# Summing four modulation rows over the partitions: matrix products with ones, or GpSimd additions with layout changes through DRAM

## The chip, the cores and the metric

The program runs on one core of one Trainium2 chip. The metric is the device time of one execution in microseconds (us), as the median of several. Before the change it is 1385.47 us, the median of 3 runs (1384.9 to 1385.56).

## What is computed

One layer of a diffusion backbone over 1024 latent tokens of width 1024, with 256 context tokens. A conditioning vector c gives six modulation rows of 1024 numbers each; two token mixers (retention and differential attention) share one input projection and one output projection; a gated MLP follows.

```python
sc = jax.nn.silu(c)
m_lat = sc @ w_mod + b_mod
sh1, sc1, g1, sh2, sc2, g2 = split(m_lat, 6)
h = rms_norm(x, norm1_g) * (1 + sc1) + sh1
y = token_mixers(h, h_ctx, w_in, ...) @ w_out
x = x + g1 * y
h2 = rms_norm(x, norm2_g) * (1 + sc2) + sh2
x = x + g2 * conv_ffn(h2, w_up, conv_w, conv_b, w_down)
return rms_norm(x, final_g)
```

The first two rows (sh1, sc1) are needed at once. This text is about the other four, the late ones: g1, sh2, sc2 and g2, numbered i = 0 to 3. Each is a product of a vector of 1024 with a matrix of 1024 x 1024.

## The kernel before

All matrix products in fp32 precision are made as three products of split operands (high x high, high x low, low x high; lines L131 to L133). A weight slice `raw` is loaded by SP's queue, ScalarE casts it to `whi` (L187), VectorE subtracts to get `wlo` (L188), and TensorE uses both.

**The stages near the change.** The input projection has seven column blocks of 512. They run in the order 6, 5, 2, 1, 3, 0, 4. Each block has four weight slices. Block 5 gives the keys of the attention (`transposed`, L450: tiles `pl`), block 2 the values of the retention (`natural`, L392: tiles `pn`, with a mean subtracted by three VectorE operations, L406 to L408), block 1 the retention keys, first for the two context tiles (`natural`, the last call before the change's new place) and then for the latents (`transposed`). `natural` leaves each tile in PSUM until ScalarE has copied it out (L403).

**The late modulation rows** are made beside blocks 5, 2 and 1 by the generator `modulations2` (L464), which is advanced from inside the matrix loops (`tick`). For each row i it loads eight tiles of weights `wm2` (128 partitions x 1024 columns) over SP's queue, with four buffers, and accumulates on VectorE: `macc = wm2 * silu(c) + macc` (L481). `macc` starts as zeros from a GpSimd memset (L478), with the bias row loaded by SP into its first partition (L479). There are two `macc` buffers. At the end `macc` holds 128 partial sums for each of 1024 columns, one for each partition.

**The sum over partitions** is `turned_sums` (L489). For i = 0 and 3 two products of a matrix of ones with `macc` (L494, `pg`, 128x512) give the summed row in all 128 partitions; ScalarE copies it out (L496) and SP stores it to DRAM as 128 equal rows (`g1_d`, `g2_d`, L497). For i = 1 and 2 eight products of `macc` with two columns of ones (L501, `pg`, 128x2) give the row as a column layout, one number for each partition and block of 128, which VectorE writes to the small tile `m2` (L503, L505, L506). Row i is summed when row i + 1 has had its fourth step; row 3 is summed at the end.

**Where the sums are used.** `g1` is loaded by GpSimd's queue during the attention (L1025) and used in the output projection; `m2` is used when the MLP's input is turned (`turned`, L1098); `g2bc` is loaded by SP's queue (L1429) and used at the end.

**What sets the order.** In these stages a scheduler lays out each engine's queue from a model of its own; each engine then runs its queue in that order and waits where an operand is late. In the attention, the order of all engines but GpSimd is written out by hand (a table of times for one unit of 128 queries and one head, 32 units), and `order_only` pins an instruction behind another. GpSimd's queue holds, besides the memsets above, nothing from the context tiles to the outputs of the retention (`score`, L246, whose first GpSimd operation is `qq`, L251), which run beside block 0.

Of the kernel before, what the change touches and what calls it, by code (L numbers as in the profile page):

```python
# [8 lines left out]
F32 = mybir.dt.float32  # L9
# [3 lines left out]
ALU = mybir.AluOpType  # L13
# [4 lines left out]
P = 128  # L18
D = 1024
KD = D // P  # L20
# [18 lines left out]
COL_N2 = 72  # L39
# [33 lines left out]
def kernel(  # L73
# [16 lines left out]
    nc = tc.nc  # L90
    mm = nc.tensor.matmul
# [17 lines left out]
    ones = kp.tile([P, P], F32, name="ones")  # L109
# [6 lines left out]
    def order_only(ins, before):  # L116
        tc.add_manual_dep(ins, before.name, mybir.DependencyInfo(mybir.DependencyClass.NoSync, mybir.DependencyReason.DATA), reason="order")
# [19 lines left out]
    g1_d = dr.tile([P, D], F32, name="g1d")  # L137
    g2_d = dr.tile([P, D], F32, name="g2d")
# [9 lines left out]
    m2 = kp.tile([P, 2, KD], F32, name="m2")  # L148
# [5 lines left out]
    with ExitStack() as p1:  # L154
# [5 lines left out]
        pst = psx.enter_context(tc.tile_pool(name="pst1", bufs=3, space=PSUM, side="right"))  # L160
# [11 lines left out]
        ev = p1.enter_context(tc.tile_pool(name="ev", bufs=2))  # L172
# [291 lines left out]
        def modulations2():  # L464

            def load(n):
                wt = m2p.tile([P, D], F32, name="wm2", bufs=4)
                tc.keep_in_program_order(nc.sync.dma_start(out=wt, in_=w_mod2[n // KD, n % KD]))
                return wt

            wts, acc, done = [], None, None
            for n in range(4 * KD + 3):
                if n < 4 * KD:
                    wts.append(load(n))
                i, k = divmod(n - 3, KD)
                if k == 0 and n >= 3:
                    done, acc = acc, m2p.tile([P, D], F32, name="macc", bufs=2)
                    nc.gpsimd.memset(acc, 0.0)  # L478
                    tc.keep_in_program_order(nc.sync.dma_start(out=acc[0:1, :], in_=rows[:, R_BMOD + (2 + i) * D : R_BMOD + (3 + i) * D]))  # L479
                if n >= 3:  # L480
                    nc.vector.scalar_tensor_tensor(out=acc, in0=wts.pop(0), scalar=csil[:, k, 0:1], in1=acc, op0=ALU.mult, op1=ALU.add)  # L481
                if k == 3 and i > 0:
                    turned_sums(i - 1, done)
                yield
            yield
            yield
            turned_sums(3, acc)

        def turned_sums(i, acc):  # L489
            if i in (0, 3):  # L490
                dst = g1_d if i == 0 else g2_d
                for n in range(2):
                    pg = pst.tile([P, 512], F32, name="pg", tag="tr")
                    mm(pg, ones, acc[:, n * 512 : (n + 1) * 512], start=True, stop=True)  # L494
                    st = ev.tile([P, 512], F32, name="st")
                    nc.scalar.copy(st, pg)  # L496
                    nc.sync.dma_start(out=dst[:, n * 512 : (n + 1) * 512], in_=st)  # L497
            else:
                pg = pst.tile([P, KD, 2], F32, name="pg2", tag="tr")
                for d in range(KD):  # L500
                    mm(pg[:, d, :], acc[:, d * P : (d + 1) * P], ones[:, 0:2], start=True, stop=True)  # L501
                if i == 1:
                    nc.vector.tensor_copy(m2[:, 0, :], pg[:, :, 0])  # L503
                else:
                    nc.vector.tensor_scalar(out=m2[:, 1, :], in0=pg[:, :, 0], scalar1=1.0, scalar2=None, op0=ALU.add)  # L505
                    nc.vector.tensor_tensor(out=m2[:, 1, :], in0=m2[:, 1, :], in1=cl[:, COL_N2 : COL_N2 + KD], op=ALU.mult)  # L506

        by_head = [(h, hf) for h in range(H) for hf in range(2)]
        m2c = p1.enter_context(ExitStack())
# [1 line left out]
        with ExitStack() as p0:  # L511
# [52 lines left out]
            part = [mm_tile("pn") for _ in range(4)]  # L564
# [95 lines left out]
            for k in range(KD):  # L660
# [28 lines left out]
                n = k + 4  # L689
# [87 lines left out]
        with tc.tile_pool(name="rc0", bufs=1) as r0:  # L777
# [20 lines left out]
            acc = r0.tile([P, 8], F32, name="acc")  # L798
# [30 lines left out]
        beside(iter(()), 0.0)  # L829
        pctx.close()  # L830
        m2c.close()
        rtab = load_rope(0)
        rtx = p1.enter_context(ExitStack())
        rt = rtx.enter_context(tc.tile_pool(name="rt", bufs=2, side="right"))
# [177 lines left out]
    with ExitStack() as p2:  # L1012
        at = p2.enter_context(tc.tile_pool(name="at", bufs=2))
        psa = p2.enter_context(tc.tile_pool(name="psa", bufs=1, space=PSUM))

        turns = {}
        start = len(nc.cur_bb.bb.instructions)
        order = sorted(TAU.items(), key=lambda it: it[1] % 1.0)
        for n in range(n_units + 8):
            if 1 < n < n_units:  # L1020
                units[n] = Unit(n)
                vars(units[n]).update(fore[n])
            if n == 9:
# [356 lines left out]
    with ExitStack() as p5:  # L1380
# [292 lines left out]
```

## Time and profile before

| | |
|---|---|
| median of 3 runs | 1385.47 us |
| the profiled execution | 1386.43 us |
| its span, first to last instruction | 1384.6 us |
| TensorE busy | 1366.8 us, 99% of the span |
| TensorE's clock in the profile | full in all 40 slices |
| VectorE, ScalarE, GpSimd busy | 998.1, 733.9, 302.0 us |
| HBM traffic | 154 GB/s over the span |

The profiled execution took 1386.43 us, 0.96 us more than the median; 1.8 us of it lie outside the span. Lines of the timeline read: start in us, duration in us, engine, line, operation, output <- inputs, shape, and in brackets how long the engine had been idle and who released it. A busy TensorE is modelled: matrix products overlap, so the distance between two starts is the cost of one and not its duration.

### The profile page before, as it was taken

To read this page: it belongs to the slowest core of one execution; us is meant where nothing else is said; L and a number is where in the kernel's file an instruction comes from. 1 tells how busy PE (TensorE), PEld (TensorE's weight loads), DVE (VectorE), ACT (ScalarE), POOL (GpSimd) and SP (SyncE) were. 2 spreads that over 40 slices of the span, in tenths; PEclk is the share of its full clock that TensorE was granted. 3 is DMA by queue.
4 is the path that set the end of the run, shared out by engine and by line. 5 is a ranking of instruction groups with operands and counts; after the bars stand their busy time and mean duration, and the time that the engine had idled before them with its cause. 6 is when DMAs were issued, how large, how long until landed. Compare 5 with 4: busy or idle time off the path is not lost.

```text
span 1384.6 us, 19518 instructions
## 1 busy us (share of the span) xinstructions
PE 1366.8 (99%) x7066; PEld 1149.8 (83%) x7066; DVE 998.1 (72%) x1474; ACT 733.9 (53%) x1400; POOL 302.0 (22%) x323
## 2 busy tenths in 40 slices
PE   9999999999999999999999999999999999999997
PEld 6788888888988799998888788888888888888886
DVE  4655874424776898896458998887778777799857
ACT  4652322434665789987136644555545555454534
POOL 1310000002666423411200643222332220000001
PEclk9999999999999999999999999999999999999999
DMA  9546885464564778622510232332323325963523
GB/s 361 215 163 209 299 269 178 144 177 147 153 190 140 217 176 184 143 52 78 190 67 24 98 109 106 114 114 92 114 99 114 107 69 178 378 226 111 179 91 122
DMA packets 95624, 214.63 MB, mean 155 GB/s; under 512 B 9316, under 2 KB 29796, under 8 KB 95016
## 3 DMA queue, kind: packets, MB, share of 16 engines
q1 hardware_dynamic: 86792, 187.03, 39.6%
q0 software_dynamic: 8160, 24.91, 7.9%
q10 hardware_dynamic: 576, 1.44, 0.3%
q8 instruction: 56, 0.92, 0.3%
q14 instruction: 40, 0.33, 0.1%
HBM read 158.03 MB, written 55.31 MB: 154 GB/s over the span
## 4 chain that ended last, share of the span: by engine, by line
PE 90%; DVE 3%; POOL 2%; ACT 2%; DMA 2%; issue 1%; POOLq 0%; SPq 0%; DVEq 0%; ACTq 0%
PE chain L131 6%; PE chain L132 6%; PE chain L133 6%; PE pv L906 5%; PE pA L874 5%; PE c L133 5%; PE c L131 5%; PE c L132 5%; PE pn L131 3%; PE pn L133 3%; PE pn L132 3%; PE pl L133 3%; PE pl L131 3%; PE pl L132 3%; PE third L131 3%; PE third L133 3%
## 5 line engine op out<-in xcount | busy, mean ns | idle before, releaser
L131 PE MATMUL pl<-hT,whi 128*128 128x512 f32 x256 | 105.7, 413 | 0.0
L131 PE MATMUL chain<-T,whi 128*128 128x512 f32 x264 | 103.0, 391 | 1.1 <-ACT ua L1306 1.1
L132 PE MATMUL chain<-T,whi 128*128 128x512 f32 x264 | 102.8, 389 | 0.0
L133 PE MATMUL chain<-T,wlo 128*128 128x512 f32 x264 | 102.4, 389 | 0.0
L133 PE MATMUL pl<-hT,wlo 128*128 128x512 f32 x256 | 100.3, 392 | 0.0
L132 PE MATMUL pl<-hT,whi 128*128 128x512 f32 x256 | 100.0, 391 | 0.0
L877 DVE TENSOR_REDUCE mt<-pA 128x1 f32<-128x1280 f32 x64 | 95.1, 1489 | 3.6 <-PE pA L874 3.2
L874 PE MATMUL pA<-ks,qhl 128*128 128x512 f32 (+1 forms) x384 | 89.7, 369 | 0.8 <-DMA ks<-dk 0.6
L131 PE MATMUL c<-whi,ghl 128*128 128x512 f32 x232 | 90.2, 389 | 0.0
L132 PE MATMUL c<-wlo,ghl 128*128 128x512 f32 x232 | 90.2, 389 | 0.0
L133 PE MATMUL c<-whi,ghl 128*128 128x512 f32 x232 | 90.2, 389 | 0.0
L881 ACT ACTIVATE p<-pA,mt 128x1280 f32<-128x1280 f32 x64 | 85.4, 1335 | 5.3 <-DVE mt L877 4.4
L1054 ACT CAST whi<-cmb 128x512 fp32r<-128x512 f32 x62 | 38.4, 622 | 81.8 <-PE chain L132 69.3
L874 PEld LDWEIGHTS pA<-ks,qhl 128*128 128x128 f32 x384 | 67.8, 189 | 13.3 <-issue 1.3
L906 PE MATMUL pv<-va,aT 128*128 128x128 f32 x640 | 77.0, 275 | 0.1
L1218 POOL TENSOR_TENSOR cmb<-wrb 128x512 f32<-128x512 f32 x19 | 27.9, 1468 | 221.9 <-DMA wrb<-w_up 168.9
L1057 DVE TENSOR_TENSOR wlo<-cmb,whi 128x512 fp32r<-128x512 f32 x62 | 60.1, 973 | 20.3 <-ACT whi L1054 20.3
L906 PEld LDWEIGHTS pv<-va,aT 128*128 128x128 f32 x640 | 74.0, 192 | 0.7 <-DVE yT L935 0.3
L1054 ACT CAST whi<-wra 128x512 fp32r<-128x512 f32 x54 | 33.2, 622 | 73.3 <-PE third L132 42.3
L131 PE MATMUL third<-yT,whi 128*128 128x512 f32 x168 | 65.4, 389 | 0.0
L132 PE MATMUL third<-yT,whi 128*128 128x512 f32 x168 | 65.4, 389 | 0.0
L133 PE MATMUL third<-yT,wlo 128*128 128x512 f32 x168 | 65.4, 389 | 0.0
(328 smaller groups left out, 3853.7 us busy)
## 6 DMA issues: line engine op xcount, KB each, us to landing
wm<-w_mod SPq DMA_DIRECT2D x32, 512.0 KB, 4.9
raw<-w_in SPq DMA_DIRECT2D x27, 512.0 KB, 4.6
wra<-w_up SPq DMA_DIRECT2D x24, 512.0 KB, 3.2
wrb<-w_up SPq DMA_DIRECT2D x22, 512.0 KB, 3.5
W<-w_down SPq DMA_DIRECT2D x44, 256.0 KB, 5.8
ad<-s SPq DMA_DIRECT2D x20, 512.0 KB, 3.5
wra<-ad SPq DMA_DIRECT2D x20, 512.0 KB, 3.4
kvs<-kvg SPq DMA_DIRECT2D x36, 256.0 KB, 3.0
```

The costliest lines, as they stand in the source:

```text
L131: mm(ps, lh, rh, start=first, stop=False, skip_group_check=more)
L132: mm(ps, lh, rl, start=False, stop=False, skip_group_check=more)
L133: return mm(ps, ll, rh, start=False, stop=last, skip_group_check=more)
L874: mm(self.pa[m][:, c0:c1], self.q[:, m, i, qs], self.k[:, m, c0:c1], start=(i == 0), stop=(i == 1))
L877: nc.vector.tensor_reduce(out=self.mt[:, m : m + 1], in_=self.pa[m][:, :LK], axis=AX.X, op=ALU.min)
L881: nc.scalar.activation(self.p[m], self.pa[m][:, :LK], AF.Exp, scale=-1.0, bias=self.mt[:, m : m + 1], accum_out=self.s[:, m : m + 1])
L906: mm(self.pv, self.aT[:, c, :], self.v[:, c, :], start=(c == 0), stop=(c == NKT - 1))
L1054: cast = nc.scalar.copy(hi, src)
L1057: nc.vector.tensor_tensor(out=lo, in0=src, in1=r32(hi), op=ALU.subtract)
L1218: nc.gpsimd.tensor_tensor(out=s1, in0=b1, in1=b2, op=ALU.add)
```

## The change

`turned_sums` goes, with its 4 + 16 matrix products, its four copies on ScalarE and its four stores on SP. In its place each finished `macc` is stored whole to DRAM by GpSimd's queue (`mod_d`, 512 KB each). After the context tiles of block 1 a new function `column_sums` runs four times, all on GpSimd: it loads `mod_d` back so that each partition holds eight of the 128 partial sums for 128 columns, adds these in three halvings (512, 256, 128 columns), stores the 128 x 128 result (`part_d`, 64 KB), loads that back with 32 partitions that hold the 16 remaining sums of 32 columns each, adds in four halvings (256 to 32), and stores the row of 1024 (`row_d`, 4 KB). For i = 1 and 2 a further DMA of single numbers brings the row into `m2`. `g1` and `g2bc` are now loaded with a broadcast of the 4 KB row to 128 partitions. The two VectorE operations that make `(1 + sc2) * norm2_g` move into the attention (unit 24 of 32).

```diff
-                    turned_sums(i - 1, done)
+                    nc.gpsimd.dma_start(out=mod_d[i - 1].rearrange("r (q b) c -> (r q) (b c)", b=KD), in_=done)
...
-            turned_sums(3, acc)
-
-        def turned_sums(i, acc):
-            if i in (0, 3):
-                dst = g1_d if i == 0 else g2_d
-                for n in range(2):
-                    pg = pst.tile([P, 512], F32, name="pg", tag="tr")
-                    mm(pg, ones, acc[:, n * 512 : (n + 1) * 512], start=True, stop=True)
-                    st = ev.tile([P, 512], F32, name="st")
-                    nc.scalar.copy(st, pg)
-                    nc.sync.dma_start(out=dst[:, n * 512 : (n + 1) * 512], in_=st)
-            else:
-                pg = pst.tile([P, KD, 2], F32, name="pg2", tag="tr")
-                for d in range(KD):
-                    mm(pg[:, d, :], acc[:, d * P : (d + 1) * P], ones[:, 0:2], start=True, stop=True)
...
+            last_mod.append(nc.gpsimd.dma_start(out=mod_d[3].rearrange("r (q b) c -> (r q) (b c)", b=KD), in_=acc))
+
+        def column_sums(i):
+            t1 = ev.tile([P, 2, 512], F32, name="t1", tag="xhl").rearrange("p a b -> p (a b)")
+            load = nc.gpsimd.dma_start(out=t1.rearrange("p (r c) -> p r c", c=P), in_=mod_d[i].rearrange("r p c -> p r c"))
+            order_only(load.ins, last_mod[0].ins)
+            for n in (512, 256, 128):
+                nc.gpsimd.tensor_tensor(out=t1[:, :n], in0=t1[:, :n], in1=t1[:, n : 2 * n], op=ALU.add)
+            nc.gpsimd.dma_start(out=part_d[i].rearrange("q (b x) c -> (q b) (x c)", b=KD), in_=t1[:, :P])
+            t2 = t1[:32, 512:]
+            nc.gpsimd.dma_start(out=t2.rearrange("p (q c) -> p q c", c=32), in_=part_d[i].rearrange("q p c -> p q c"))
+            for n in (256, 128, 64, 32):
+                nc.gpsimd.tensor_tensor(out=t2[:, :n], in0=t2[:, :n], in1=t2[:, n : 2 * n], op=ALU.add)
+            nc.gpsimd.dma_start(out=row_d[i], in_=t2[:, :32])
+            if i in (1, 2):
+                nc.gpsimd.dma_start(out=m2[:, i - 1, :], in_=row_d[i].rearrange("(d u) j -> (u j) d", u=4))
...
         pctx.close()
         m2c.close()
+        for i in range(4):
+            column_sums(i)
...
-                    nc.gpsimd.dma_start(out=g1, in_=g1_d)
+                    nc.gpsimd.dma_start(out=g1, in_=row_d[0].rearrange("p c -> (p c)").partition_broadcast(P))
...
+    plus_one = nc.vector.tensor_scalar(out=m2[:, 1, :], in0=m2[:, 1, :], scalar1=1.0, scalar2=None, op0=ALU.add)
+    order_only(plus_one.ins, turns["M0", n_units - 8])
+    nc.vector.tensor_tensor(out=m2[:, 1, :], in0=m2[:, 1, :], in1=cl[:, COL_N2 : COL_N2 + KD], op=ALU.mult)
...
-        nc.sync.dma_start(out=g2bc, in_=g2_d)
+        nc.sync.dma_start(out=g2bc, in_=row_d[3].rearrange("p c -> (p c)").partition_broadcast(P))
```

**How the queues move.** The scheduler lays the queues out anew. In TensorE's queue the 20 products go; the one other difference lies in the context tiles of block 1. There `pn_2014` (before) or `pn_1996` (after) is the first context tile and `pn_2043` or `pn_2025` the second; `whi_2010`, `wlo_2011` (after: `whi_1992`, `wlo_1993`) are the two halves of the block's fourth weight slice. Before:

```order
L133 MATMUL pn_2014<-whi_2004,cT1_625 128x512
L131 MATMUL pn_2014<-whi_2010,cT0_624 128x512
L131 MATMUL pn_2043<-whi_1992,cT0_624 128x512
L132 MATMUL pn_2043<-wlo_1993,cT0_624 128x512
L133 MATMUL pn_2043<-whi_1992,cT1_625 128x512
L131 MATMUL pn_2043<-whi_1992,cT0_624 128x512
L132 MATMUL pn_2043<-wlo_1993,cT0_624 128x512
L132 MATMUL pn_2014<-wlo_2011,cT0_624 128x512
```

After:

```order
L133 MATMUL pn_1996<-whi_1986,cT1_635 128x512
L131 MATMUL pn_1996<-whi_1992,cT0_634 128x512
L131 MATMUL pn_2025<-whi_1974,cT0_634 128x512
L132 MATMUL pn_1996<-wlo_1993,cT0_634 128x512
L133 MATMUL pn_1996<-whi_1992,cT1_635 128x512
```

Five products of the second tile stood between the first use of the fourth slice's high half and the first use of its low half; now one stands there.

On VectorE, the same weight slice is split in the midst of the last `macc` row. `mu` and `st` with the operations at L406 to L408 (after: L407 to L409) are the mean subtraction of block 2's last two tiles. Before:

```order
L481 SCALAR_TENSOR_TENSOR macc_1855<-wm2_1835,csil_177,macc_1855 128x1024
L406 TENSOR_REDUCE mu_1951<-st_1949 128x4
L481 SCALAR_TENSOR_TENSOR macc_1855<-wm2_1853,csil_177,macc_1855 128x1024
L407 TENSOR_SCALAR mu_1951<-mu_1951 128x4
L188 TENSOR_TENSOR wlo_2005<-raw_2002,whi_2004 128x1024
L481 SCALAR_TENSOR_TENSOR macc_1855<-wm2_1879,csil_177,macc_1855 128x1024
L408 TENSOR_TENSOR st_1949<-st_1949,mu_1951 128x512
L481 SCALAR_TENSOR_TENSOR macc_1855<-wm2_1894,csil_177,macc_1855 128x1024
L406 TENSOR_REDUCE mu_1985<-st_1983 128x4
L481 SCALAR_TENSOR_TENSOR macc_1855<-wm2_1917,csil_177,macc_1855 128x1024
L407 TENSOR_SCALAR mu_1985<-mu_1985 128x4
L188 TENSOR_TENSOR wlo_2011<-raw_2008,whi_2010 128x1024
```

After:

```order
L482 SCALAR_TENSOR_TENSOR macc_1847<-wm2_1804,csil_187,macc_1847 128x1024
L407 TENSOR_REDUCE mu_1933<-st_1931 128x4
L482 SCALAR_TENSOR_TENSOR macc_1847<-wm2_1827,csil_187,macc_1847 128x1024
L408 TENSOR_SCALAR mu_1933<-mu_1933 128x4
L189 TENSOR_TENSOR wlo_1987<-raw_1984,whi_1986 128x1024
L482 SCALAR_TENSOR_TENSOR macc_1847<-wm2_1845,csil_187,macc_1847 128x1024
L409 TENSOR_TENSOR st_1931<-st_1931,mu_1933 128x512
L482 SCALAR_TENSOR_TENSOR macc_1847<-wm2_1871,csil_187,macc_1847 128x1024
L407 TENSOR_REDUCE mu_1967<-st_1965 128x4
L482 SCALAR_TENSOR_TENSOR macc_1847<-wm2_1886,csil_187,macc_1847 128x1024
L408 TENSOR_SCALAR mu_1967<-mu_1967 128x4
L189 TENSOR_TENSOR wlo_1993<-raw_1990,whi_1992 128x1024
```

From the reduction of the second last tile to the fourth slice's low half the kinds of the operations are the same; the row of `macc` as a whole stands one step earlier.

On GpSimd, the place between the last memset and the first operation of the retention's outputs was empty. Before:

```order
L478 MEMSET macc_1217 128x1024
L478 MEMSET macc_1394 128x1024
L478 MEMSET macc_1684 128x1024
L478 MEMSET macc_1855 128x1024
L251 TENSOR_TENSOR qq_2933<-st_2902,qd_871 128x512
```

After, the beginning of what stands there now (`t1` is the tile of the first additions; from the first load of `t1` to the last DMA into `m2` it is 46 rows, and `qq` follows behind them):

```order
L479 MEMSET macc_1847 128x1024
L484 DMA mod2_85<-macc_1685 128x1024
L488 DMA mod3_86<-macc_1847 128x1024
L494 DMA t1_2056<-mod0_83 128x8x128
L494 DMA t1_2068<-mod1_84 128x8x128
L497 TENSOR_TENSOR t1_2056<-t1_2056 128x512
L497 TENSOR_TENSOR t1_2056<-t1_2056 128x256
L497 TENSOR_TENSOR t1_2056<-t1_2056 128x128
L498 DMA part0_87<-t1_2056 128x128
```

The rows go through in two pairs: 0 and 1 together, then 2 and 3 in the same two buffers.

More of the change, by code (lines that the diff above doesn't have):

```diff
@@ L136 @@
     kvg_d = [dr.tile([P, H, 3, 2, P], F32, name=f"kvg{g}") for g in range(NKT // 2)]
-    g1_d = dr.tile([P, D], F32, name="g1d")
-    g2_d = dr.tile([P, D], F32, name="g2d")
+    mod_d = [dr.tile([8, P, P], F32, name=f"mod{i}") for i in range(4)]
+    part_d = [dr.tile([16, 32, 32], F32, name=f"part{i}") for i in range(4)]
+    row_d = [dr.tile([32, 32], F32, name=f"row{i}") for i in range(4)]
     dq_d = [dr.tile([64, 2, 2, L], F32, name=f"dq{h}") for h in range(H)]
@@ L486, in modulations2 @@
             yield
-            turned_sums(3, acc)
-        def turned_sums(i, acc):
-            if i in (0, 3):
-                dst = g1_d if i == 0 else g2_d
-                for n in range(2):
-                    pg = pst.tile([P, 512], F32, name="pg", tag="tr")
-                    mm(pg, ones, acc[:, n * 512 : (n + 1) * 512], start=True, stop=True)
-                    st = ev.tile([P, 512], F32, name="st")
-                    nc.scalar.copy(st, pg)
-                    nc.sync.dma_start(out=dst[:, n * 512 : (n + 1) * 512], in_=st)
-            else:
-                pg = pst.tile([P, KD, 2], F32, name="pg2", tag="tr")
-                for d in range(KD):
[L501 to L506, printed above, removed]
+            last_mod.append(nc.gpsimd.dma_start(out=mod_d[3].rearrange("r (q b) c -> (r q) (b c)", b=KD), in_=acc))
+        last_mod = []
+        def column_sums(i):
[12 more added lines that the diff above has]
+                nc.gpsimd.dma_start(out=m2[:, i - 1, :], in_=row_d[i].rearrange("(d u) j -> (u j) d", u=4))
         by_head = [(h, hf) for h in range(H) for hf in range(2)]
```

## Prediction, on record before the run

> **What bounds the kernel now.** I read the page's busy shares first, then a table by stretches around the change, then TensorE's timeline at the four sums, and last the engines and queues that the change loads.
>
> ```profile
> PE 1366.8 (99%) x7066; PEld 1149.8 (83%) x7066; DVE 998.1 (72%) x1474; ACT 733.9 (53%) x1400; POOL 302.0 (22%) x323
> PE 90%; DVE 3%; POOL 2%; ACT 2%; DMA 2%; issue 1%; POOLq 0%; SPq 0%; DVEq 0%; ACTq 0%
> ...
> 120.00:150.00 30.00, 30.00 (x132) 24.52 (x131) 24.84 (x31) 11.99 (x20) 0.00 (x0) 1.00 0.71 240
> 150.00:175.00 25.00, 25.00 (x119) 20.66 (x118) 17.82 (x23) 4.62 (x8) 0.96 (x1) 1.00 0.90 310
> 175.00:200.00 25.00, 25.00 (x120) 20.97 (x120) 18.44 (x25) 4.50 (x6) 0.96 (x1) 1.00 0.77 258
> 200.00:225.00 25.00, 25.00 (x108) 20.00 (x108) 16.23 (x19) 6.73 (x9) 0.00 (x0) 1.00 0.83 257
> 225.00:250.00 25.00, 25.00 (x120) 20.71 (x119) 7.93 (x12) 7.41 (x13) 0.00 (x0) 1.00 0.38 131
> ```
>
> In the stretches the columns are the length, then PE, PE's weight loads, VectorE, ScalarE and GpSimd with their instruction counts, the granted clock, the DMA engines' share and GB/s. TensorE has no gap in any stretch in which the sums stand, at clock 1.00; the chain that ended last is 90% TensorE. GpSimd does almost nothing there. DMA is the second load: 0.71 to 0.90 up to 225 us. So the bound is TensorE's queue, and a product taken out of it should shorten the program by its slot, unless something else is late at once.
>
> **The change part by part.**
>
> *The products removed.* TensorE's timeline at the four sums, first and last rows of the third and fourth only:
>
> ```profile
> 148.79 0.40 PE L133 MATMUL pl<-hT,wlo 128*128 128x512 f32 x1
> 149.03 1.88 PE L494 MATMUL pg<-macc,ones 128*128 128x512 f32 x4
> 150.34 0.80 PE L131 MATMUL pn<-whi,cT 128*128 128x512 f32 x1
> 150.98 0.39 PE L132 MATMUL pn<-wlo,cT 128*128 128x512 f32 x1
> 151.21 0.39 PE L133 MATMUL pn<-whi,cT 128*128 128x512 f32 x1
> ...
> 153.93 0.39 PE L133 MATMUL pn<-whi,cT 128*128 128x512 f32 x1
> ...
> 172.97 0.39 PE L133 MATMUL pn<-whi,hT 128*128 128x512 f32 x1
> 173.19 1.84 PE L501 MATMUL pg<-ones,macc 128*128 128x2 f32 x16
> ...
> 175.22 0.40 PE L132 MATMUL pn<-wlo,hT 128*128 128x512 f32 x1
> ...
> 197.93 0.39 PE L133 MATMUL pn<-whi,hT 128*128 128x512 f32 x1
> ...
> 200.19 0.40 PE L132 MATMUL pn<-wlo,hT 128*128 128x512 f32 x1
> ...
> 219.50 0.40 PE L133 MATMUL pn<-whi,cT 128*128 128x512 f32 x1
> ...
> 221.69 0.39 PE L132 MATMUL pl<-hT,whi 128*128 128x512 f32 x1
> ```
>
> An ordinary product takes (153.93 - 151.21) / 12 = 0.227 us of the queue. From the last product before a sum to the second one behind it two slots would pass, 0.45 us. It is 2.19, 2.25, 2.26 and 2.19 us, so the four sums displace 1.74, 1.80, 1.81 and 1.74: **7.09 us** together. [...] All of it is on the path, since TensorE waits for nothing here. ScalarE's four copies, SP's four stores and VectorE's three small operations go too; none of them was waited for.
>
> *What is late next: the fourth slice of block 1.* Before the second 128x512 sum TensorE needs `wlo` of that slice from VectorE, whose queue is full there:
>
> ```profile
> 203.65 0.60 ACT L403 ACTIVATE st<-pn 128x512 f32<-128x512 f32 x1 [6.69 <-PE pn L133]
> ...
> 204.28 0.69 DVE L406 TENSOR_REDUCE mu<-st 128x4 f32<-128x512 f32 x1
> ...
> 212.14 1.22 DVE L188 TENSOR_TENSOR wlo<-raw,whi 128x1024 fp32r<-128x1024 f32 x1
> ...
> 208.84 0.39 PE L131 MATMUL pn<-whi,cT 128*128 128x512 f32 x1
> ```
>
> VectorE's run from the reduction at 204.28, which starts as ScalarE has copied out a tile, to the end of `wlo` at 213.36 takes 9.08 us. The order after shows the same kinds of operations in that run, so it stays 9.08 us behind a copy that follows TensorE's progress. TensorE takes this `wlo` as its 25th product of the context tiles before, at 208.84 + 24 x 0.227 = 214.28, 0.92 us after it is ready. After, four fillers fewer stand ahead of it: 0.92 - 4 x 0.227 = 0.01 us of slack. Handing over costs something, so I take **+0.1 us** for a stall here; its bounds are 0 and, if VectorE's run is stretched by late `wm2` weights, some 2 us (each of its four `macc` steps may wait for a load). Ahead of it, VectorE no longer waits at the first steps of the last `macc` row for TensorE's third sum, which gives those loads a lead.
>
> *The waits that are new.* GpSimd's third memset waited for the first sum; now it waits for the store of `macc` 0, and SP's bias row, with every weight load queued on SP behind it, waits for the memset. The fourth does the same for `macc` 1.
>
> ```profile
> 140.31 1.28 DVE L481 SCALAR_TENSOR_TENSOR macc<-wm,csil,macc 128x1024 f32<-128x1024 f32 x1
> ...
> 150.97 0.96 POOL L478 MEMSET macc<- 128x1024 f32 x1 [71.79 <-PE pg L494]
> ...
> 167.35 0.30 SPq L479 DMA_DIRECT2D macc<-rows  x1
> ...
> wm<-w_mod SPq DMA_DIRECT2D x32, 512.0 KB, 4.9
> lg<-rows SPq DMA_DIRECT2D x1, 4.0 KB, 5.3
> woraw<-w_out POOLq DMA_DIRECT2D x4, 256.0 KB, 3.3
> DMA to landing us min/median/max: 8.9/10.0/12.7
> L953 POOL DMA_DIRECT2D qhl<-dq x18 | 11.6, 647 | 0.0
> ```
>
> `macc` 0 is complete at 141.59. A DMA issue on GpSimd takes 0.65 us (last row); a load of the same size lands after 4.9 us (`wm`); the slowest GpSimd DMA of this shape, `va` in the attention (the row of three numbers), took 12.7. So the memset runs at 147 to 155, and SP's row went at 167.35: hidden with 12 us to spare, cost **0**. Without that cover each microsecond late would stop SP's queue and then TensorE's weights.
>
> *Traffic.* Up to 225 us the stores of `macc` add about 1 MB net to some 20 MB (258 to 310 GB/s over 75 us), 5% more, where the share is 0.77 to 0.90. TensorE waits for no weights in these stretches, so 0 here but for the slack above.
>
> *The additions and their chain.* They stand between the last `macc` and `qq`:
>
> ```profile
> 331.43 2.56 POOL L251 TENSOR_TENSOR qq<-st,qd 128x512 f32<-128x512 f32 x2 [155.38 <-DVE st L433]
> ...
> L1218 POOL TENSOR_TENSOR cmb<-wrb 128x512 f32<-128x512 f32 x19 | 27.9, 1468 | 221.9 <-DMA wrb<-w_up 168.9 <-DMA ad<-tconv 36.2 <-DVE wlo L1057 16.8
> L280 POOL TENSOR_TENSOR y<-o 128x256 f32<-128x256 f32 x16 | 12.6, 788 | 24.7 <-DVE o L278 24.7
> ...
> 213.88 1.28 DVE L481 SCALAR_TENSOR_TENSOR macc<-wm,csil,macc 128x1024 f32<-128x1024 f32 x1
> ```
>
> By the two GpSimd rows an addition takes 0.11 us and 2.66 ns a column: 1.47, 0.79, 0.45 (estimate) and then 0.79, 0.45, 0.28, 0.19, 4.4 us a row, 17.6 us in all. The 19 issues take 19 x 0.65 = 12.3 us. The last `macc` ends at 215.16, less the three sums gone before it (5.35 us): 209.8. Two pairs of rows with four landings each make eight landings in series, bounded by 3.3 us (`woraw`) and 12.7. With 5.3 us, the 4 KB row `lg`, nearest to the small DMAs here, the chain ends at 209.8 + 29.9 + 42 = 282; `qq` comes at 331.43 - 7.09 = 324.3. Hidden, cost **0**.
>
> [...]
>
> *What the chain's DMAs may disturb.* At the end of block 1 TensorE waits for a load:
>
> ```profile
> 266.33 4.33 DMA raw<-w_in
> ...
> 273.74 0.63 PE L444 MATMUL pk<-ident,xa 128*128 128x128 f32 x4 [0.92 <-DVE xa L433]
> ```
>
> The load holds ScalarE, VectorE's `wlo` and the `xa` queued behind it, and with that TensorE. After the change it runs at about 259 to 264, and the chain's last DMAs (two of them of 1024 single numbers) may be under way. Bounds: 0 and, if the load takes as long as the 8.9 us `va`, 4.6 us. I take **+0.3**, near the low end, since GpSimd's DMAs come singly here and the DMA share is 0.38 in the stretch after 225.
>
> *The two operations in the attention.* `m2` is ready near 282 us and they run near 600, so they wait for nothing; they cost VectorE what its old form cost:
>
> ```profile
> 200.04 0.17 DVE L505 TENSOR_SCALAR m<-pg 128x8 f32<-128x8 f32 x1 [1.42 <-PE pg L501]
> ...
> 604.67 1.49 DVE L877 TENSOR_REDUCE mt<-pA 128x1 f32<-128x1280 f32 x1 [0.16 <-PE pA L874]
> ```
>
> Twice 0.17 us, against a wait of 0.16 us for TensorE in a unit there: 0 to 0.4 us, taken **+0.1**. The broadcast loads of `g1` and `g2bc` move the same bytes into SBUF as before and are issued long before use: 0.
>
> *Sum.* -7.09 + 0.1 + 0.3 + 0.1 = -6.6 us. The profiled execution's 1386.43 becomes 1379.8; it lies 0.96 above the median, so the median becomes **1378.9 us**.
>
> **The rivals.**
>
> *A. A later wait takes part of it.* The slack of 0.01 us at `wlo`, or the load at 266: 2 to 5 us of the 7.09 are given back, 1380.5 to 1383.5. For it: both places sit at the edge of TensorE's path. Against: each needs DMAs to run slower than their rows.
>
> *B. The products' slots come back as waits (no change).* If TensorE's pace in blocks 5, 2 and 1 were set by the weights, they would arrive no sooner and the time would stay at 1385.5. Against: TensorE stands without a gap and its spacing is 0.227 us throughout; for it, only the DMA share of 0.90.
>
> *C. GpSimd's chain ends behind `qq` (slower).* GpSimd's queue is in order, so `qq`, and with it the outputs of the retention on TensorE, waits for the last addition and the last DMA issue. The point is reached when a landing takes (324.3 - 209.8 - 29.9) / 8 = 10.6 us in the mean. At 12.7 the chain ends at 341, `qq` is 17 us late, and the time is 1378.9 + 17 = 1396; at 11.5 it is 7 us late, 1386. For it: `va` took 8.9 to 12.7, though among a burst of other loads. Against: everything else here lands in 3.3 to 5.3.
>
> **How the numbers follow.** The forecast (a gain of 5 to 7.3 us) has 0.70, A 0.13, B 0.08, C 0.09. The range runs from 1377.8, a little under the full 7.09, to 1383.0, which takes in the bounds of `wlo` and most of the load's, and leaves out B, C and the end of A. What a measurement of this kernel can tell from no change is about 0.2%, 2.8 us: faster means under 1382.7. Faster gets the forecast and most of A, 0.82; within 0.2% gets B and the rest of A and C's start, 0.09; slower 0.09.
>
> **What would show it.** In the changed profile no `pg` row is left on TensorE, and the distance across each of the four places is 0.227 us a product. At the fourth slice of block 1 a wait of TensorE for `wlo` would be 0 to 0.2 us. The memsets of `macc` come before 155 and 175. The last addition ends near 280 and `qq` near 324.5 is still released by VectorE. From there every stage stands some 6.5 us earlier to the end. Wrong would be: a gap on TensorE at `wlo` or behind 259 of microseconds (A), the same times at 250 as before (B), or `qq` released by a DMA on GpSimd (C).

## The result and the profile after

The changed kernel takes **1381.55 us**, the median of 20 runs (1379.84 to 1385.09), against 1385.47 (1384.59 to 1386.94, 20 runs) for the kernel before on the same chip: ratio 0.9976, 95% interval 0.9970 to 0.9982. The gain is 3.9 us where 6.6 was forecast, and the runs, which lay within 2.4 us before, now lie 5.2 us apart. The profiled execution took 1381.66 us.

First the page and the table by stretches, the lines that answer to those of the prediction (columns as there: PE, its weight loads, VectorE, ScalarE, GpSimd, clock, DMA share, GB/s):

```profile
PE 1360.5 (99%) x7026; PEld 1144.5 (83%) x7026; DVE 999.8 (72%) x1473; ACT 731.7 (53%) x1396; POOL 336.6 (24%) x373
```

```profile
150.00:175.00 25.00, 25.00 (x112) 20.68 (x111) 20.84 (x28) 4.48 (x7) 0.54 (x1) 1.00 0.98 327
175.00:200.00 25.00, 25.00 (x112) 20.71 (x111) 17.83 (x23) 4.32 (x7) 1.49 (x2) 1.00 0.91 309
200.00:225.00 25.00, 24.09 (x107) 19.63 (x106) 15.18 (x18) 5.76 (x8) 5.98 (x8) 1.00 0.86 291
225.00:250.00 25.00, 24.93 (x121) 20.35 (x119) 8.06 (x12) 7.88 (x14) 17.96 (x25) 1.00 0.67 203
```

TensorE is no longer without a gap in 200 to 225 (24.09 of 25.00), and the DMA engines carry more in every stretch: 0.98, 0.91, 0.86 and 0.67 where they had 0.90, 0.77, 0.83 and 0.38.

TensorE's timeline at the fourth slice of block 1 and at three later places:

```profile
207.37 0.61 PE L131 MATMUL pn<-whi,cT 128*128 128x512 f32 x2
208.89 0.50 PE L132 MATMUL pn<-wlo,cT 128*128 128x512 f32 x1 [0.91 <-DVE wlo L189]
...
215.15 0.39 PE L133 MATMUL pn<-whi,cT 128*128 128x512 f32 x1
...
215.60 0.39 PE L132 MATMUL pl<-hT,whi 128*128 128x512 f32 x1
...
268.19 0.63 PE L445 MATMUL pk<-ident,xa 128*128 128x128 f32 x4 [1.16 <-DVE xa L434]
...
462.32 0.88 PE L895 MATMUL pt<-ident,p 128*128 128x128 f32 x6 [1.44 <-DVE xa L432]
```

Where the fourth sum stood, the distance is 215.60 - 215.15 = 0.45 us, two slots, in place of 2.19: the products are gone. The product that began at 221.69 begins at 215.60, 6.09 us earlier and not 7.09: the wait of 0.91 for `wlo` stands ahead of it. The `pk` that began at 273.74 is 5.55 us earlier (its wait was 0.92 and is 1.16), and the span ends 4.7 us earlier. So one microsecond is lost at `wlo`, and the rest in pieces of a few tenths behind it.

Why `wlo` is late is on ScalarE and VectorE, here ScalarE first:

```profile
199.13 0.60 ACT L404 ACTIVATE st<-pn 128x512 f32<-128x512 f32 x1 [3.45 <-DMA kvg<-st]
```

```profile
199.77 0.68 DVE L407 TENSOR_REDUCE mu<-st 128x4 f32<-128x512 f32 x1
...
207.62 1.22 DVE L189 TENSOR_TENSOR wlo<-raw,whi 128x1024 fp32r<-128x1024 f32 x1
```

VectorE's run from the reduction to the end of `wlo` takes 208.84 - 199.77 = 9.07 us, as before (9.08). It starts late because ScalarE's copy starts late; and that copy, which before waited for TensorE (6.69 us, released by `pn`), now waits for a store: there are two `st` tiles, and the older is still on its way to DRAM (`kvg<-st`). This store takes about as long as before (7.1 us from issue to landing, 6.9 before), but it is issued only 1.3 us earlier (191.92, before 193.24), though three sums worth 5.35 us are gone ahead of it: the copies and stores in front of it were held up already (three copies, at 168.90, 176.38 and 187.65, had waited 8.33, 4.88 and 5.27 us for stores of `kvg`). Which transfer held them up first stays open.

The chain on GpSimd, and `qq` behind it:

```profile
212.13 0.53 POOL L488 DMA_DIRECT2D mod<-macc  x1 [23.16 <-DVE macc L482]
212.76 1.81 POOL L494 DMA_DIRECT2D t<-mod  x2
220.90 2.97 POOL L497 TENSOR_TENSOR t<-t 128x512 f32<-128x512 f32 x3 [6.32 <-DMA t<-mod]
...
259.72 0.93 POOL L505 DMA_DIRECT2D m<-row  x1
326.35 2.56 POOL L252 TENSOR_TENSOR qq<-st,qd 128x512 f32<-128x512 f32 x2 [65.70 <-DVE st L434]
```

It ends at 260.65, with 65 us to spare before `qq`.

### The profile page after: what moved, and what is told of

Read it like the earlier page. It is cut to its first block, busy times and chain, and to the rows that moved or that the text cites. A ratio compares the mean times of both kernels' runs of the same rounds, so it can differ in the third digit from the quotient of the medians.

```text
span 1379.9 us, 19500 instructions
## 1 busy us (share of the span) xinstructions
PE 1360.5 (99%) x7026; PEld 1144.5 (83%) x7026; DVE 999.8 (72%) x1473; ACT 731.7 (53%) x1396; POOL 336.6 (24%) x373
## 3 DMA queue, kind: packets, MB, share of 16 engines
q10 hardware_dynamic: 576, 1.44, 0.3%
## 4 chain that ended last, share of the span: by engine, by line
PE 77%; ACT 1%; DMA 1%; issue 1%; DVE 1%; POOL 1%; SPq 0%; POOLq 0%; ACTq 0%; DVEq 0%
PE chain L131 6%; PE chain L132 6%; PE chain L133 6%; PE c L132 5%; PE c L131 5%; PE pA L875 5%; PE c L133 5%; PE pv L907 5%; PE third L133 3%; PE third L132 3%; PE third L131 3%; PE pl L133 2%; PE pt L895 2%; PE pl L131 2%; PE pl L132 2%; PE po L133 2%
```

## The theories

Four theories stood for the missing 3 us. **T1:** the slack of `wlo` went with the filler products, and only for that reason do late transfers cost anything there. **T2:** the later chain of loads and additions costs it. **T3:** the time comes back at the attention's entry wherever the stages ahead of it end earlier. After the first four runs **T4** was added: the added transfers delay the kernel's own transfers, and cost time at whatever place these are needed, whatever TensorE does.

## The experiments

All ran beside the kernel before, which took 1385.6 to 1385.9 us there.

| kernel | median (range), runs | ratio, 95% interval |
|---|---|---|
| e1 the change again | 1382.86 (1380.09 to 1387.36), 11 | 0.9981 (0.9972 to 0.9991) |
| e2 no sums | 1381.28 (1380.43 to 1381.52), 6 | 0.9966 (0.9954 to 0.9978) |
| e3 stores only | 1382.38 (from 1381.35), 11 | 0.9977 (0.9968 to 0.9986) |
| e4 pinned | 1382.93 (1381.03 to 1385.85), 11 | 0.9982 (0.9974 to 0.9991) |
| e5 before, with the traffic | 1399.10 (1398.48 to 1400.35), 4 | 1.0098 (1.0085 to 1.0111) |
| e6 no sums, clean | 1380.42 (1380.29 to 1383.33), 5 | 0.9970 (0.9958 to 0.9981) |
| e7 stores only, clean | 1382.52 (1379.73 to 1388.14), 12 | 0.9981 (0.9971 to 0.9990) |
| e8 late chain | 1382.67 (1380.87 to 1387.28), 11 | 0.9979 (0.9970 to 0.9988) |
| e9 pinned and late | 1379.35 (1378.60 to 1381.95), 5 | 0.9959 (0.9946 to 0.9971) |
| e10 before, with the traffic in place | 1389.32 (1388.29 to 1390.71), 7 | 1.0028 (1.0017 to 1.0039) |
| e11 before again | 1385.59 (1384.32 to 1386.31), 11 | 1.0000 (0.9991 to 1.0008) |
| e12 as e9 | 1379.86 (1379.17 to 1380.94), 5 | 0.9960 (0.9946 to 0.9973) |

One run of e3 took 5458 us; nothing explains it, and without it the median would be 0.2 us lower.

**e1, the change again.**

> The changed kernel once more, as it stands, to have its time beside the other three on one chip. Every theory expects the result again: 1381.5 us, within 1380 to 1383, 3 to 5 us less than the kernel before. Its trace should again show the wait of about 0.9 us for wlo of block 1's fourth slice at about 209 us if that wait is a fixed part of the change; if it is set by transfers that land by chance, it will differ by some tenths.

Measured: 1382.86, and a spread of 7.3 us. Its profiled execution is the longest of its runs (1387.36), and shows what such a run has. TensorE's timeline behind `wlo`:

```profile
207.01 0.61 PE L131 MATMUL pn<-whi,cT 128*128 128x512 f32 x2
210.49 0.50 PE L132 MATMUL pn<-wlo,cT 128*128 128x512 f32 x1 [2.87 <-DVE wlo L189]
...
211.40 0.63 PE L132 MATMUL pn<-wlo,cT 128*128 128x512 f32 x1
211.82 0.63 PE L133 MATMUL pn<-whi,cT 128*128 128x512 f32 x1
...
214.38 0.48 PE L131 MATMUL pn<-whi,cT 128*128 128x512 f32 x1
214.70 0.40 PE L132 MATMUL pn<-wlo,cT 128*128 128x512 f32 x1
```

```profile
200.00:225.00 25.00, 22.14 (x91) 17.82 (x90) 14.57 (x16) 6.09 (x9) 4.35 (x5) 0.93 0.93 305
```

The same wait is 2.87 us here, so it is not of a fixed length: the two ScalarE copies ahead of VectorE's run wait 7.20 and 3.01 us, both released by stores of `kvg`, and run at 196.51 and 200.12 (195.08 and 199.13 in the profile of the change), and the run starts at 201.19 (199.77). And behind it TensorE's products stand 0.43 us apart instead of 0.227 from 211.40 to 214.38; the granted clock of the stretch is 0.93. Seven products at 0.2 us more each make a further 1.4 us: this wait is paid one and a half times, 2.87 + 1.4 = 4.3 us. The pace is a little over half of the usual one (0.227 / 0.43 = 0.53) for 3.0 us; what sets it off the trace does not show.

**e2 and e3, the parts of the change.** e3 leaves out the chain (the loads, the additions and the layout changes) and keeps the stores of `macc`; e2 leaves out the stores too. The four rows are taken from the biases alone. How `m2` is filled in both, and one of the stores that e2 takes away:

```diff
             if i in (1, 2):
-                nc.gpsimd.dma_start(out=m2[:, i - 1, :], in_=row_d[i].rearrange("(d u) j -> (u j) d", u=4))
+                c = R_BMOD + (2 + i) * D
+                nc.gpsimd.dma_start(out=m2[:, i - 1, :], in_=rows[0, c : c + D].rearrange("(d j) -> j d", j=P))
...
-                    nc.gpsimd.dma_start(out=mod_d[i - 1].rearrange("r (q b) c -> (r q) (b c)", b=KD), in_=done)
```

> The four sums are left out whole: no stores of the products, no GpSimd additions, no layout changes; the four rows are taken from the biases alone, so the part of the products is missing from them. TensorE, VectorE and ScalarE keep the changed kernel's order. This is the change without its traffic and without its GpSimd work. Theory T1 (the loss is the fourth slice of block 1, which has no slack left, made worse by the traffic of the macc stores): 1378.5 to 1380, with a wait for wlo of at most 0.3 us. Theory T2 (the loss is the later chain of loads and additions on GpSimd): 1378.5 to 1379.5. Theory T3 (the time comes back at the attention's entry wherever the stage ahead of it ends earlier): 1381 to 1382, like the changed kernel.

> The four stores of macc to DRAM stay, the chain behind them (loads, additions, layout changes) is left out, and the rows come from the biases alone. T1: like the changed kernel up to 240 us, so 1380.5 to 1382, with the wait for wlo of 0.9 us there. T2: like the kernel with no sums, 1378.5 to 1379.5. T3: 1381 to 1382.

Measured: 1381.28 and 1382.38. Both were spoiled by the edit: the loads of single numbers into `m2` depended on nothing, went to the head of GpSimd's queue and ran in the opening, where the DMA engines are close to full (share 0.90 or more from 5 to 20 us in e2). The waits of TensorE in e2:

```profile
PE pr L512 <- DMA wt<-w_mod: 0.9, 1, 0.9
```

This row (total, times, longest) is only in e2 and, with 1.1, in e3. What stands is that e2 has no wait for `wlo` though its order is the changed kernel's, and e3 has 0.9 us of it.

**e4, the wait for `wlo` alone.**

```diff
+        fourth = low_halves[-1]
...
+        for step in steps[-5:]:
+            order_only(step.ins, fourth.ins)
```

> The whole change, with one thing added: on VectorE the last five additions of the products for macc are held behind wlo of block 1's fourth slice, so that this subtraction no longer waits its turn. T1: the wait for wlo at 209 us goes and 0.7 to 1.2 us come back: 1380.3 to 1380.9, about 1 us below the changed kernel on the same chip. T2 and T3: within 0.3 us of the changed kernel, 1381.5; the wait that goes there comes back at a later place.

Measured: 1382.93, the same as e1 on that chip. The wait for `wlo` is gone from its profile, and another stands further on. The profile is of a long run (1385.50); what the five runs of 1381 to 1382 us lost is not seen in it. GpSimd, SyncE's queue, ScalarE and TensorE, one fence each:

```profile
215.92 1.82 POOL L496 DMA_DIRECT2D t<-mod  x2
```

```profile
218.00 0.52 SPq L412 DMA_DIRECT2D kvg<-st  x1
226.49 0.33 SPq L230 DMA_DIRECT2D kvs<-kvg  x1
```

```profile
229.83 0.91 ACT L317 ACTIVATE ks<-kvs,kd 128x256 f32<-128x256 f32 x2 [9.43 <-DMA rk<-xa]
```

```profile
234.69 1.11 PE L447 MATMUL pk<-ident,xa 128*128 128x128 f32 x4 [4.84 <-DVE xa L436]
235.46 0.78 PE L131 MATMUL pl<-hT,whi 128*128 128x512 f32 x1
236.03 0.63 PE L132 MATMUL pl<-hT,whi 128*128 128x512 f32 x1
236.46 0.63 PE L133 MATMUL pl<-hT,wlo 128*128 128x512 f32 x1
```

Read from below: TensorE waits for `xa`, VectorE for ScalarE's copies `xb`, which are queued behind `ks`. By the code `ks` reads `kvs` (the bracket names `rk<-xa`, a transfer issued just behind it on the same queue). The first load of `kvs` can go only when the last store of `kvg` has landed, since it reads the same rows. The store was issued at 218.00 and the load at 226.49: 8.5 us for a transfer of 256 KB, while the two loads of `t`, 512 KB each, issued from 215.92 on, are under way. The same distance is 7.7 us in the profile of the change and 6.0 in e1. It is 2.5 to 4.6 us in the nine profiles in which no load of `t` runs there (before, e2, e3, e6 to e9, e11, e12). The clock falls behind this wait too (0.93 in 225 to 250, the products 0.43 us apart from 236.03).

So T1 as it stood fails: `wlo` is not the one place. In the profile of the change `kvs` was late as well (ScalarE idled 4.82 us in front of `ks`, which began at 227.03), but no wait of TensorE followed: there TensorE came to its first `pk` 1.8 us later than in e4 (225.58 against 223.77), and `ks` began 2.8 us earlier. That the wait at `wlo` hides this place fits these two profiles; it is argued from them.

**e5 and e10, the traffic with the sums left on TensorE.** All that the change adds stands beside the old sums, its result unused (e5). In e10 the unused copy of `m2` lies in an existing tile:

```diff
-    pad(kp, 96)
+    spare = kp.tile([P, 24], F32, name="pad", bufs=1)
+    nc.vector.memset(spare, 0.0)
+    m2x = spare[:, : 2 * KD].rearrange("p (a d) -> p a d", a=2)
```

> The kernel before, its four sums still on TensorE, with all that the change adds laid beside it and its result unused: the four stores of macc, the loads, the additions, the layout changes. TensorE, VectorE, ScalarE and SyncE keep the order of before. Theory T4 (the added transfers delay the kernel's own transfers, whatever TensorE does): 1.0 to 2.5 us above the kernel before, 1386.5 to 1388, and a spread of several us between runs. Theory T1 (the transfers cost only since the slack of block 1's fourth slice went with the products): within 0.4 us of the kernel before, 1385.2 to 1386, spread about 2 us.

> e5 once more with its one flaw taken out: the 64 bytes that the unused copy of m2 takes lie inside a tile that the kernel before has already, so no other tile's address moves. In e5 TensorE's products ran 1 to 3 per cent slower from 800 us to the end, which gave 8 us of its 13.4. If that came from the moved addresses, those 8 us go: 1386.5 to 1390 (T4: the traffic alone costs 1 to 4 us, with a spread of several us), or 1385.2 to 1386 (T1: no cost while the slack is there). If it came from the traffic, the time stays at 1399.

Measured: 1399.10 and 1389.32. The first is mostly something else. Two stretches of e5, then the same of e10:

```profile
900.00:930.00 30.00, 30.00 (x133) 24.62 (x132) 20.67 (x26) 14.42 (x21) 11.41 (x8) 1.00 0.28 105
...
1320.00:1350.00 30.00, 30.00 (x130) 24.17 (x129) 12.25 (x15) 11.38 (x15) 0.00 (x0) 1.00 0.30 99
```

```profile
900.00:930.00 30.00, 30.00 (x134) 24.86 (x133) 22.74 (x27) 15.54 (x23) 9.35 (x7) 1.00 0.28 106
...
1320.00:1350.00 30.00, 30.00 (x135) 24.82 (x134) 14.28 (x19) 10.56 (x17) 0.00 (x0) 1.00 0.32 104
```

In e5 133 and 130 products go through where e10 has 134 and 135, at the same clock and about the same DMA share: the 64 bytes by which e5 had moved every later tile made TensorE's products 1% and 3 to 4% longer there. From the first product of `third` to the last of `c` e5 takes 617.2 us and e10 608.7. With the addresses in place these 8.5 us of the 9.8 between the two are gone. The change itself has no such loss: the same stretch takes 608.7 us in the kernel before and in the changed one.

What is left in e10, 3.5 us over the kernel before (interval 2.4 to 5.4), is the price of the traffic with the old slack at `wlo` in place. So T4 holds against T1. Its place is beside that of e4:

```profile
224.34 0.59 ACT L503 COPY st<-pg 128x512 f32<-128x512 f32 x1 [4.37 <-DMA kvg<-st]
...
229.60 0.91 ACT L319 ACTIVATE ks<-kvs,kd 128x256 f32<-128x256 f32 x2 [2.71 <-DMA kvs<-kvg]
```

```profile
230.83 0.39 PE L135 MATMUL pl<-hT,wlo 128*128 128x512 f32 x1
234.21 0.63 PE L449 MATMUL pk<-ident,xa 128*128 128x128 f32 x4 [2.99 <-DVE xa L438]
234.59 0.48 PE L133 MATMUL pl<-hT,whi 128*128 128x512 f32 x1
234.91 0.40 PE L134 MATMUL pl<-hT,whi 128*128 128x512 f32 x1
```

ScalarE's first copy of the fourth sum waits 4.37 us for a store of `kvg` to land. In the kernel before it ran at 220.84, here at 224.34, and what follows it (the second copy, the load of `kvs`, `ks`) is 3.1 to 3.3 us later than before. The wait at `ks` itself is no longer than before (2.71 and 2.53). These copies are not in the changed kernel, so e10 shows that the traffic costs time with the slack at `wlo` in place, and not how much of it the changed kernel pays.

(TensorE stood from 230.83 to 234.21 and its clock did not fall, 1.00 in 225 to 250; in e1 it fell behind a wait of 2.87 us. What decides it is not the length of the gap alone.)

**e6 and e7, e2 and e3 without their flaw.** `m2` is set to zero by GpSimd:

```diff
-                nc.gpsimd.dma_start(out=m2[:, i - 1, :], in_=rows[0, c : c + D].rearrange("(d j) -> j d", j=P))
+                nc.gpsimd.memset(m2[:, i - 1, :], 0.0)
```

> As e2, with the two rows of m2 set to zero by GpSimd in place of the two loads of single numbers that in e2 ran in the first 15 us and held a load of w_mod back by 0.9 us (the products' part of all four rows is left out, and the bias of two). It gives what the removal of the sums alone is worth: 1380.2 to 1380.6, 0.7 to 0.9 us under e2, with a spread of 1 us. If it gives 1378.5 to 1379, the loss of e2 was larger than its profile showed.

> As e3, with m2 set to zero by GpSimd in the same way: the removal of the sums, with the four stores of macc and without the chain behind them. T4 with the cost in the stores: 1381.3 to 1381.7, 1 us over e6. T4 with the cost in the chain's loads: 1380.2 to 1380.7, like e6.

Measured: 1380.42, as expected, and 1382.52, 0.8 us more than the upper bound given for it; the stores alone cost 2.1 us by the medians (with five runs of e6 the two intervals overlap) and bring back the spread. In e6 the step at `wlo` goes as the prediction had it. VectorE, then TensorE:

```profile
198.47 0.68 DVE L407 TENSOR_REDUCE mu<-st 128x4 f32<-128x512 f32 x1
...
206.32 1.22 DVE L189 TENSOR_TENSOR wlo<-raw,whi 128x1024 fp32r<-128x1024 f32 x1
```

```profile
207.59 0.50 PE L132 MATMUL pn<-wlo,cT 128*128 128x512 f32 x1
```

Without the stores the run of 9.07 us ends at 207.54, and the product follows at 207.59 with no wait worth a bracket; in e7's profile it waits 2.4 us. The five profiles with the stores and without e4's pins (the change, e1, e3, e7, e8) all have a wait here, of 0.9 to 2.9 us; the two without the stores (e2, e6) have none. The fillers that went are thus not enough to cost the microsecond; with the stores they do. T2 is not the whole cause either, since e7 has the loss without the chain.

e6 has two kinds of runs, three at 1380.3 to 1380.4 and two at 1383.2 and 1383.3. Its profile is one of the latter and shows the difference. ScalarE and TensorE in e6:

```profile
400.55 1.04 ACT L188 CAST whi<-raw 128x1024 fp32r<-128x1024 f32 x1 [6.13 <-DMA raw<-w_in]
```

```profile
403.21 0.46 PE L331 MATMUL pu<-kvs,ks 128*128 128x128 f32 x2 [3.34 <-ACT jk L272]
```

A weight load there takes 7.3 us from issue to landing and not 4.8 as in the profile after, ScalarE stands in front of it, and TensorE waits 3.34 us. e7's profile has it too. Why this load is late in some runs stays open; none of the added transfers is near it.

**e8, the chain held back; e9 and e12, with e4's pins.**

```diff
-            order_only(load.ins, last_mod[0].ins)
+            tc.add_manual_dep(load.ins, turned_last[0].ins.name, mybir.DependencyInfo(mybir.DependencyClass.Sync, mybir.DependencyReason.DATA), reason="late")
...
-        for i in range(4):
-            column_sums(i)
         rtab = load_rope(0)
...
         transposed(wg, rk_d, rtab, 64, RET_SCALE, 0, by_head, True)
+        for i in range(4):
+            column_sums(i)
```

> The whole change, with the chain held until VectorE has finished the last rotated pass of block 1 (about 265 us), so that its 2 MB of loads no longer fall on the first loads of kvs at 222 us and the load of raw at 258. It then runs from 265 to about 315 us, ahead of qq at 326. T4 with the cost in the chain: 1380.5 to 1381.3, 1 to 2 us under the changed kernel, with a smaller spread. T4 with the cost in the stores: like the changed kernel, 1381.5 to 1383. If the chain runs past 326 us, slower than that.

> The whole change with both additions of e4 and e8: the last five additions for macc behind wlo of block 1's fourth slice, and the chain held until the last rotated pass of block 1. In e4 the wait for wlo went, but the profile had a gap of 5.2 us on TensorE at 230, where ScalarE waited for the first loads of kvs while the loads of t ran; in e8 those loads were moved away, and the wait for wlo stayed, 1.4 us. If these two places carry the loss (T4, at two places), both go here: 1380.3 to 1381.3, with a spread of 2 to 3 us, and no gap over 1 us on TensorE between 200 and 262. If the late transfers come out at whatever place is next (T4, at no fixed place), the time is that of e4 and e8, 1382 to 1383, with the gap somewhere else.

> e9 once more, for more runs of it: e4 and e8 alone gave 1382.93 and 1382.67, both together 1379.35 in five runs. If the two places carry the loss together, again 1379 to 1380, ratio to the kernel before 0.995 to 0.9965. If e9 was a lucky draw from the spread of the changed kernel (1380 to 1387), 1381 to 1383.

Measured: e8 1382.67, no gain by itself, with 1.4 us at `wlo` in its profile. e9 1379.35 and e12 1379.86; the ten runs of both lie between 1378.60 and 1381.95. Both medians lie below the 1380.3 that stood as the lower bound for e9. Each remedy alone gives nothing, both together some 3 us (1382.86 for e1 and 1379.86 for e12 on one chip): with the pins alone `kvs` comes too late for TensorE, with the late chain alone TensorE still stands at `wlo`. The profile of e9, SyncE's queue and the stretches:

```profile
216.75 0.52 SPq L412 DMA_DIRECT2D kvg<-st  x1
220.94 0.33 SPq L230 DMA_DIRECT2D kvs<-kvg  x1
```

```profile
200.00:225.00 25.00, 25.00 (x114) 20.70 (x113) 15.40 (x19) 6.39 (x11) 0.54 (x1) 1.00 0.80 271
225.00:250.00 25.00, 25.00 (x119) 20.66 (x118) 7.93 (x12) 8.59 (x15) 0.00 (x0) 1.00 0.39 131
```

The load of `kvs` now goes 4.2 us after the store of `kvg` (8.5 in e4), TensorE has no gap in either stretch, and the DMA share of 225 to 250 is 0.39 again. The chain runs while block 3 is made, and is done before `qq`:

```profile
266.37 1.81 POOL L496 DMA_DIRECT2D t<-mod  x2 [51.84 <-DVE xa L436]
...
310.02 0.93 POOL L507 DMA_DIRECT2D m<-row  x1
323.83 2.56 POOL L254 TENSOR_TENSOR qq<-st,qd 128x512 f32<-128x512 f32 x2 [12.88 <-DVE st L436]
```

This version beats both kernels: it is 6.0 to 6.5 us under the kernel before, by medians. Against the change as it was the ratios are 0.996 to 0.9976 and 0.9981, some 2 to 3 us; their intervals touch, but eight of these ten runs take 1380.70 us or less, and four of the 31 runs of the change do. T3 fails with it: the gain of the early stages goes through the attention's entry nearly whole.

**e11, the kernel before again.**

> The kernel before, for a second profile of it beside the others. Every theory expects 1385.6, spread 2 us, and no gap on TensorE of over 1.8 us between 60 us and the end, as in its first profile; a gap of over 2.7 us followed by products at 0.43 us would show that such gaps are not the change's own.

Measured: 1385.59, spread 2.0, no gap over 1.6 us behind 60 us in its profile. Long waits on TensorE, and the fall of the clock behind them, came with the change and its parts and not with the kernel before, in the two profiles that there are of it.

## Why the prediction came out as it did

*The products removed, 7.09 us:* right. The distance at the fourth place fell from 2.19 to 0.45 us, and where the two later waits are taken away (e9, e12) 6.0 to 6.5 us of it reach the end. In the profile of e9 nothing is lost at first: from the first product of `pl` to the first `pk` it takes 223.88 - 93.33 = 130.55 us, the kernel before 231.66 - 93.96 = 137.70, so 7.15 us less.

*The fourth slice of block 1, +0.1 us:* the working was right (slack about 0, VectorE's run 9.07 us, 0.05 us from its end to the product, as e6 shows), but its start was wrong. It took ScalarE's copy to follow TensorE; with the stores of `macc` it follows the landing of `kvg`, and the wait is 0.9 us in one profile of the change and 2.9 in the other. The second lies above the bound of 2 us, which was given for another cause, late weights `wm2` during VectorE's run.

*Traffic, 0:* this is the step that failed: "TensorE waits for no weights in these stretches, so 0 here but for the slack above." The traffic costs 3.5 us in e10, there by way of the copies of the fourth sum, and some 3 us of the change come back in e9 and e12. The amount was too small as well: by the GB/s of the two tables 2.5 MB more went through from 150 to 225 us, not 1. The chain's first two loads, 1 MB, were left out, though the prediction's own sum starts them at 209.8. And the step looked at loads that TensorE waits for, and not at the stores whose buffers ScalarE needs, nor at the pair of store and load (`kvg`, `kvs`) that ScalarE waits for at 226. The second was to be seen in the profile before:

```profile
226.31 0.91 ACT L314 ACTIVATE ks<-kvs,kd 128x256 f32<-128x256 f32 x2 [2.53 <-DMA kvs<-kvg]
```

ScalarE idled 2.53 us in front of `ks` there, and TensorE, which needs the copies behind it, just did not wait for them. From the issue of the last store of `kvg` to that of the first load of `kvs` it takes 8.5 us in e4 and 7.7 in the changed kernel, with the loads of `t` under way, and 4.2 in e9 and 2.6 in the kernel before, without them. How the two share the DMA engines was not shown.

*The new waits on stores of `macc`, 0, and the chain ahead of `qq`, 0:* right. The memsets ended at 145.9 and 176.5, and SyncE's bias rows behind them went at 167.9 and 191.6. The chain ended at 260.65 where 282 was worked out. The sum was not right in its parts: the first two loads of `t` took 8.1 and 9.4 us to land, longer than its 5.3, and the small transfers behind them 1.6 to 4.6 us, shorter than it, the two rows of a pair partly side by side.

*The chain's DMAs at the load `raw`, +0.3:* `pk` waits 1.16 us there in place of 0.92, but the second profile of the kernel before (e11) has 0.4, so the size cannot be told; the place was not the one that counts. The chain's first two loads, not its last small ones, do harm, some 30 us earlier.

*The two operations in the attention, +0.1:* no run isolates them. The wait for `xa` at the attention's entry is 1.44 us where it was 1.04; but it is 1.0 in e6 and e9 and 1.4 in e10, which keeps the sums, so it does not follow the removal of the sums.

*The rivals:* A, a later wait that takes 2 to 5 us of the gain, is what happened, 3.9 us being left of 7.09. Its first place was named, its second was not, and the objection to it, that DMAs would have to run slower than their rows, is what came true. B and C did not come: no slot came back as a wait for weights, and `qq` is released by VectorE. The forecast itself, a gain of 5 to 7.3 us with a chance of 0.70, did not come either. That 1381.55 lies within 1377.8 to 1383.0 is because the range took in most of rival A, which had a chance of 0.13; it does not bear out the sum.

## What to carry to other kernels

Before traffic is added to stretches as busy as these (a DMA share of 0.77 to 0.90 from 150 to 225 us), follow the chains that pass through a store: a buffer that is free only when its store has landed, and a load that reads what a store has just written. In the kernel before, the pair of `kvg` and `kvs` carried no idle time on TensorE, which came late enough; it showed only as 2.53 us on ScalarE. And where two waits stand one behind the other, as `wlo` and `kvs` did here, each remedy alone can read as nothing (e4 1382.93 and e8 1382.67, beside 1382.86 for e1) where both together took off some 3 us (e12 1379.86); try both together before either is dropped.

## What the runs showed of the hardware

- A wait of 2.9 us on TensorE was followed by products at 0.43 us instead of 0.227 for 3 us (e1). The same followed a wait of 4.84 us in e4, one of 2.36 us in e7 and one of 3.34 us in e6. In e10 TensorE stood from 230.83 to 234.21 and the products behind it came at 0.23 us. In the profiles of the kernel before and of the change, where the longest waits are 1.2 and 1.44 us, the clock is 1.00 in every stretch of 20 us from 40 to 1360 us, and in e8, with 1.4 us at `wlo`, it is 1.00 in 200 to 225.
- With the later tiles moved by 64 bytes in SBUF (e5), 133 and 130 products went through in the 30 us from 900 and from 1320 us, and 134 and 135 without the move (e10): 8.5 us in all. Which operand's address does it was not tried.
- Two DMAs of 1024 single numbers, 4 KB each, issued in the opening from 1.30 us on, landed after 7.6 us (e2, the median). TensorE waited 0.9 us there for a load of `w_mod`; in e6, which has memsets in place of these two DMAs, there is no such wait.
